# Splitting low parts on VectorE alone: GpSimd leaves tensor work in a two-layer attention, convolution and expert kernel

## The chip, the cores and the metric

The kernel runs on one core of a Trainium2 chip. The metric is the device time of one execution in microseconds, the median over runs. A change of under 0.2% (some 3.7 us) can hardly be told from no change.

## What is computed

Two layers over 256 tokens of width 1024, all in fp32. Each layer is a mixer (attention over one block of 256 keys and a gated convolution of width 3, their outputs gated, added and projected) and a mixture of single-vector experts (product keys, top 16 of 16384 experts for each of 8 heads). Every normalization has a scale and a shift that come from a vector `c`.

```python
for l in range(DEPTH):
    ada = (c @ w_ada[l] + b_ada[l])[:, None, :]
    sh1, sc1, g1, sh2, sc2, g2 = jnp.split(ada, 6, axis=-1)
    h = rmsnorm(x, norm1_g[l]) * (1.0 + sc1) + sh1
    q, k, v, b_gate, c_gate, hc, gate_a, gate_c = jnp.split(h @ w_in[l], SPLIT_POINTS, axis=-1)
    merged = (jax.nn.sigmoid(gate_a) * (moba_attention(q, k, v, slopes) @ w_attn_proj[l])
              + jax.nn.sigmoid(gate_c) * (gated_short_conv(b_gate, c_gate, hc, conv_w[l]) @ w_conv_proj[l]))
    x = x + g1 * (merged @ w_out[l])
    h = rmsnorm(x, norm2_g[l]) * (1.0 + sc2) + sh2
    x = x + g2 * peer(h, w_query[l], sub_keys[l], expert_u[l], expert_v[l])
return rmsnorm(x, final_g)
```

## The kernel before

**Order.** Everything is emitted by hand in one order (`manual_schedule`), and each engine takes its own instructions in that order, with semaphores between engines. All weights form one list, `stream`, of 1 MB groups of two units. `load_ahead` (L175) issues the groups on the SyncE queue, in order, as soon as a buffer is free: five buffers `raw0` for the first 13 groups, then a ring of three buffers `raw`, and in the expert stages parts of other tiles too.

**Mixers.** A mixer multiplies in two parts: each weight unit `raw` (128x1024) is split into a high part `wh`, written by ScalarE (L340), and a low part `wl = raw - wh` (L345); the activations are split into `hh` and `hl` likewise. TensorE then does three products, `wh*hh`, `wh*hl` and `wl*hh` (`step`, L392, and `across`, L818). `next_unit` (L311) prepares one unit, up to four units ahead of TensorE. `l_engine` (L304) says which engine takes the low part:

```python
pol["acc"] += pol["pool"]
if pol["acc"] >= 0.999:
    pol["acc"] -= 1.0
    return G
return V
```

So a share of 0.5 gives GpSimd (G) every second unit and VectorE (V) the rest. Between the weight groups `stream` holds groups of `w_ada`, which go to no matrix product: VectorE multiplies each unit with `c` and sums (L288), or adds it up with a factor (L285).

The first mixer begins with `first_norm` (L517), where the order is `START = "cuuccvcuccvcc"`: c is a pair of L288 units that ends in one column block of scale and shift, u and v are weight groups. After each c, `shift` (L531) lets ScalarE write `hh` and then `z`, and the low part `hl` is their difference (L536). In the second layer `norm` (L584) does this (L624). The stages of a mixer: query, key and value products, convolution, gates (L780), the projections (L797 to L801), the output product (`across`).

**Experts.** Tokens 0 to 127 go dense through all experts (`U` by L1099, `V` by L1157), with weights from one-hot factors: `onehots` (L1060) writes `q = (j == jT)` on VectorE (L1068) and multiplies it with `gT` (L1069), ScalarE writes `p`, TensorE multiplies (L1086), and VectorE applies the result (L1088). Four tokens are one batch, and a batch is used two batches after it is made. Tokens 128 to 255 fetch their expert rows one by one with indirect DMAs on the GpSimd queue (L991), and VectorE takes each row in (L1007, L1015).

At the end of a layer `finish_block` and `rstd` (L491) update `x` and work out its norms with a row of tiny VectorE instructions (L484 to L489); between them `next_unit` prepares the first units of the next layer.

Of the kernel before, what the change touches and what calls it, by code (L numbers as in the profile page):

```python
# [14 lines left out]
OP = mybir.AluOpType  # L15
# [4 lines left out]
KD = D // 128  # L20
# [4 lines left out]
TB = 4  # L25
# [10 lines left out]
WARM = (3, 6, 6)  # L36
LEAD = 4

POOL_START, POOL_MIX, POOL_PROJ = 0.5, (0.6, 0.4), 0.34


def f(ap):
    return ap.bitcast(F32)
# [3 lines left out]
def body(ctx: ExitStack, tc: tile.TileContext, d: dict, out: bass.AP):  # L47
    nc = tc.nc
    V, A, G, T = nc.vector, nc.scalar, nc.gpsimd, nc.tensor
# [20 lines left out]
    def w_ps(shape):  # L70
        return psum.tile(shape, F32, name="wp", bufs=2)

    def y_ps(shape):
        return psum.tile(shape, F32, name="yp", bufs=4)
# [227 lines left out]
    pol = {"pool": 0.0, "acc": 0.0}  # L302
# [78 lines left out]
    def unit(kind):  # L381
        n = AHEAD + (2 if more["pool"] is not None and kind != "out" else 0)
        while len(ready) < n + 1 and next_unit():
            pass
        return take(kind)

    def take(kind):
        k, h, lo = ready.popleft()
        assert k == kind, (k, kind)
        return h, lo  # L390
# [109 lines left out]
    def rms_row(between=lambda: None):  # L500

        dg = work.tile([128, NT, 128], F32, name="dg")
        y = rstd()
        for t in range(NT):
            if t:
                A.activation(dg[:, t], ident, AF.Copy, scale=y[:, t:t + 1])
            else:
                V.tensor_scalar(dg[:, t], ident, y[:, t:t + 1], None, op0=OP.mult)
        ps = y_ps([128, S])
        for t in range(NT):  # L510
            T.matmul(ps[:, t * 128:(t + 1) * 128], ones, dg[:, t], start=True, stop=True)
        between()
        rr = dg.rearrange("p t c -> p (t c)")
        V.tensor_copy(rr, ps)
        return rr

    def first_norm(xps):  # L517


        rr = rms_row(lambda: [next_unit() for _ in range(2)])  # L520
        for j in range(KD // 2):
            V.tensor_tensor(xh[:, 2 * j:2 * j + 2], xps[j], rr[:, None].to_broadcast([128, 2, S]), op=OP.mult)
        hh = split["h"].tile([128, KD, S], F32R, name="hh")
        hl = split["h"].tile([128, KD, S], F32R, name="hl")
        n = NFIRST[0]
        ws, reach, nv = [], [], 0
        pss = [(y_ps if i < 4 else mm_ps)([128, S]) for i in range(n)]
        vp = [w_ps([128, 512]) for _ in range(NT)]
        k = 0

        def shift(k):  # L531
            a, b = acol[:, 0, 0, k:k + 1], adac[:, 0, 0, k:k + 1]
            z = work.tile([128, S], F32, name="hf", bufs=4)
            A.activation(hh[:, k], xh[:, k], AF.Identity, bias=b, scale=a)
            A.activation(z, xh[:, k], AF.Identity, bias=b, scale=a)
            (V if k == KD - 1 else G).tensor_tensor(hl[:, k], z, f(hh[:, k]), op=OP.subtract)  # L536

        def products(nu, nk):
            new = [(i, x) for i in range(nu) for x in range(reach[i], nk)]
            for i, x in new:  # L540
                h, lo = (w[:, x * 128:(x + 1) * 128] for w in ws[i])
                T.matmul(pss[i], h, hh[:, x], start=(x == 0), stop=False)
                T.matmul(pss[i], lo, hh[:, x], start=False, stop=False)
            for i, x in new:
                h = ws[i][0][:, x * 128:(x + 1) * 128]
                T.matmul(pss[i], h, hl[:, x], start=False, stop=(x == KD - 1))
                reach[i] = x + 1

        todo = []
        while k < KD or len(ws) < n:  # L550
            for fn in todo:
                fn()
            todo = []
            next_unit()
            if ready and ready[0][0] == "qk":
                ws.append(take("qk"))
                reach.append(0)
            while k < KD and (0, 0, k) in done:
                shift(k)
                k += 1  # L560
            todo.append(lambda a=len(ws), b=k: products(a, b))
            while ready and ready[0][0] == "v" and k >= 2 * nv + 2:
                todo.append(lambda w=take("v"), u=nv: v_unit(vp, hh, hl, *w, u))
                nv += 1
        for fn in todo:
            fn()
        while nv < 4:
            v_unit(vp, hh, hl, *unit("v"), nv)
            nv += 1
        for _ in range(AHEAD + 1):  # L570
            next_unit()
        return hh, hl, pss, vp

    def v_unit(vp, hh, hl, h, lo, u):
        for kk in range(2):
            k = 2 * u + kk
            for t in range(NT):
                ts = slice(t * 128, (t + 1) * 128)
                c = slice(kk * 512, (kk + 1) * 512)
                T.matmul(vp[t], hh[:, k, ts], h[:, c], start=(k == 0), stop=False)  # L580
                T.matmul(vp[t], hh[:, k, ts], lo[:, c], start=False, stop=False)
                T.matmul(vp[t], hl[:, k, ts], h[:, c], start=False, stop=(k == KD - 1))

    def norm(l, w, kind, xps):  # L584

        rr = rms_row()
        keep_warm(WARM[2])
        hh = split["h"].tile([128, KD, S], F32R, name="hh")
        hl = split["h"].tile([128, KD, S], F32R, name="hl")
        ws, pss = [], []  # L590

        def products(k, low):
            if not ws:
                while len(ready) < 2:
                    next_unit()
                ws.extend(take(kind) for _ in range(2))
                pss.extend(y_ps([128, S]) for _ in range(2))
            c = slice(k * 128, (k + 1) * 128)
            for (h, lo), ps in zip(ws, pss):
                if low:  # L600
                    T.matmul(ps, h[:, c], hl[:, k], start=False, stop=(k == KD - 1))
                else:
                    T.matmul(ps, h[:, c], hh[:, k], start=(k == 0), stop=False)
                    T.matmul(ps, lo[:, c], hh[:, k], start=False, stop=False)

        def shift(k):
            z = work.tile([128, S], F32, name="hf", bufs=4)
            V.scalar_tensor_tensor(z, xps[k // 2][:, k % 2], acol[:, l, w, k:k + 1], rr, op0=OP.mult, op1=OP.mult)
            b = adac[:, l, 2 * w, k:k + 1]
            if k == 0:  # L610
                V.tensor_scalar(hh[:, k], z, b, None, op0=OP.add)
            else:
                A.activation(hh[:, k], z, AF.Identity, bias=b)
                if k % 2:
                    A.activation(z, z, AF.Identity, bias=b)
            return z, b

        zs = deque()
        for k in range(KD):
            while len(zs) < LEAD and k + len(zs) < KD:  # L620
                zs.append(shift(k + len(zs)))
            z, b = zs.popleft()
            if k % 2:
                G.tensor_tensor(hl[:, k], z, f(hh[:, k]), op=OP.subtract)  # L624
            else:
                V.scalar_tensor_tensor(hl[:, k], z, b, f(hh[:, k]), op0=OP.add, op1=OP.subtract)
            products(k, False)
            if k:
                products(k - 1, True)
        products(KD - 1, True)  # L630
        return hh, hl, pss
# [17 lines left out]
    def mixer(pool, l, hh, hl, pss, vp=None):  # L649
# [157 lines left out]
        for k in range(KD - 2):  # L807
# [3 lines left out]
                warm_sqrt()  # L811
            across(ys, mh[:, k], ml[:, k], h, lo, k == 0, False)
            tick()
        pol["pool"] = 1.0
        more["pool"] = None
        return finish(pool, ys, row, "out", [(mh[:, k], ml[:, k]) for k in (KD - 2, KD - 1)])

# [138 lines left out]
    def experts(es, xp, rp, low, halves, pairs, hot, l, hf, pss):  # L956
# [8 lines left out]
        gT = xp.tile([128, 128], F32, name="gT")  # L965
# [94 lines left out]
        def onehots(half, b):  # L1060


            x = b % 3
            p = hot[:, 2 * x:2 * x + 2].rearrange("p a b -> p (a b)").rearrange("p (t i) -> p t i", t=TB)
            q = hot[:, 6 + x].rearrange("p (t j) -> p t j", t=TB)
            ts = slice(b * TB, b * TB + TB)
            all_j = iotf[:, None, 64 * half:64 * half + 64].to_broadcast([128, TB, 64])
            V.tensor_tensor(q, all_j, jT[:, ts, None].to_broadcast([128, TB, 64]), op=OP.is_equal)  # L1068
            G.tensor_tensor(q, q, gT[:, ts, None].to_broadcast([128, TB, 64]), op=OP.mult)  # L1069
            for i in range(TB):  # L1070
                A.activation(p[:, i], iotf, AF.Abs, bias=iT[:, b * TB + i:b * TB + i + 1])  # L1071
            A.activation(p, p, AF.Relu, bias=1.0, scale=-1.0)
            return p, q
# [60 lines left out]
        for e in range(0, NE, 2):  # L1134
# [33 lines left out]
            if e == LAST:  # L1168
                assert not flying
                finish_block(1, 0)  # L1170
        pol["pool"] = 1.0
        finish_block(0, 0)
        if not xg:
            while len(ready) < 2 and next_unit():
# [110 lines left out]
```

## Time and profile before

| | |
|---|---|
| median of 3 runs | 1861.13 us (1859.49 to 1862.21) |
| the profiled execution's own time | 1862.17 us |
| its span, from the first instruction to the last | 1860.4 us |
| busy in the span | TensorE 1608.0, VectorE 1398.7, ScalarE 575.4, GpSimd 945.4 us |
| moved by DMA | 669.24 MB, mean 360 GB/s |

The two layers are at 0 to 945 and 945 to 1860 us. In each, a mixer of 210 to 250 us is followed by the query product (65 us), the U stage, of which the last 110 us have the one-hot weighting, and the V stage (300 us). PE is TensorE, DVE is VectorE, ACT is ScalarE, POOL is GpSimd, SP is SyncE, whose queue issues the weight loads. Busy time of an engine counts every instruction from its start to its end.

### The profile page before, as it was taken

The numbers are of one execution on the slowest core, as the hardware profiler recorded it, in microseconds if no ns is written. First come the engines' busy times: TensorE is split into PE (matmuls) and PEld (weight loads), VectorE is DVE, ScalarE is ACT, GpSimd is POOL, SyncE is SP. The second block draws the span as 40 slices with busy tenths as digits, with TensorE's granted clock in tenths as the row PEclk, the third lists the DMA queues.
The fourth block names the chain that finished last, engine by engine and source line by source line (L and its number), as shares of the span: only waits on it lengthen the run. The fifth ranks groups of instructions, "written<-read, shape, count | busy, mean of one in ns | idle before, by whom it ended". The sixth has DMA issues, their size and how long they took to land.

```text
span 1860.4 us, 26229 instructions
## 1 busy us (share of the span) xinstructions
PE 1608.0 (86%) x9527; PEld 1260.9 (68%) x9527; DVE 1398.7 (75%) x2681; ACT 575.4 (31%) x1257; POOL 945.4 (51%) x731
## 2 busy tenths in 40 slices
PE   6799989986789989887789999998786998898776
PEld 4788878986789644532357997898785994444222
DVE  7797859999988767654565877699997887666455
ACT  3464332111166433300046443221113653431001
POOL 3435204444589777755341231244446987776551
PEclk7899999988989999999999999999898999999998
DMA  8668788999999999999945677899999999999996
GB/s 318 249 227 298 295 341 298 408 409 409 408 391 395 411 415 415 415 415 415 397 178 199 252 291 263 328 377 408 409 408 394 392 404 416 414 415 412 416 416 271
DMA packets 163203, 669.24 MB, mean 360 GB/s; under 512 B 16001, under 2 KB 16001, under 8 KB 146690
## 3 DMA queue, kind: packets, MB, share of 16 engines
q1 hardware_dynamic: 87346, 396.39, 54.3%
q0 software_dynamic: 73856, 268.48, 36.4%
q10 hardware_dynamic: 1872, 2.69, 0.4%
q8 instruction: 75, 1.23, 0.3%
q14 instruction: 54, 0.44, 0.1%
HBM read 666.46 MB, written 1.05 MB: 359 GB/s over the span
## 4 chain that ended last, share of the span: by engine, by line
DVE 31%; DMA 27%; PE 24%; issue 8%; POOL 6%; ACT 3%; SPq 0%; POOLq 0%; DVEq 0%; ACTq 0%
DMA rows<-in_expert_v_dram,idx 15%; PE mm L1099 8%; DVE rows L1007 7%; DMA raw<-in_expert_v_dram 6%; PE yp L1157 4%; POOL rows L991 4%; PE wp L1086 3%; DVE raw L288 3%; DVE y L1015 3%; DMA rows<-in_expert_rows_dram,idx 2%; DVE wl L345 2%; PE mm L394 2%; PE mm L395 1%; PE mm L396 1%; ACT wh L340 1%
## 5 line engine op out<-in xcount | busy, mean ns | idle before, releaser
L991 POOL DMA_INDIRECT rows<-in_expert_rows_dram,idx x256 | 305.6, 1194 | 335.4 <-DVE rows L1007 90.4
L991 POOL DMA_INDIRECT rows<-in_expert_v_dram,idx x256 | 329.9, 1289 | 234.2 <-DMA rows<-in_expert_v_dram,idx 97.5
L1015 DVE SCALAR_TENSOR_TENSOR y<-rows,cv,y 128x1024 f32<-128x1024 f32 x254 | 335.1, 1319 | 146.8 <-DMA rows<-in_expert_v_dram,idx 140.4
L1007 DVE SCALAR_TENSOR_TENSOR rows<-rows,h 128x1024 f32<-128x1024 f32 x256 | 328.7, 1302 | 0.4 <-DMA rows<-in_expert_rows_dram,idx 0.3
L1157 PE MATMUL yp<-raw,ah 128*128 128x512 f32 x512 | 238.9, 613 | 60.6 <-DMA raw<-in_expert_v_dram 59.4
L345 POOL TENSOR_TENSOR wl<-raw,wh 128x1024 fp32r<-128x1024 f32 x52 | 136.1, 2622 | 267.0 <-ACT wh L340 255.4
L1157 PE MATMUL yp<-raw,al 128*128 128x512 f32 x512 | 241.1, 614 | 33.8 <-DMA raw<-in_expert_v_dram 33.0
L1099 PE MATMUL mm<-hfull,raw 128*128 128x128 f32 x1984 | 239.9, 280 | 20.0 <-ACT al L1113 16.8
L1099 PEld LDWEIGHTS mm<-hfull,raw 128*128 128x128 f32 x1984 | 231.1, 195 | 20.9 <-ACT al L1113 17.2
L1071 ACT ACTIVATE hot<-iotf,iT 128x128 f32<-128x128 f32 x512 | 163.2, 390 | 263.3 <-PE wp L1086 217.5
L1157 PEld LDWEIGHTS yp<-raw,ah 128*128 128x128 f32 x512 | 94.7, 193 | 203.2 <-DMA raw<-in_expert_v_dram 103.9
L1099 PE MATMUL mm<-hfull,ah 128*128 128x128 f32 x1600 | 192.8, 282 | 13.5 <-ACT al L1113 13.5
L1099 PEld LDWEIGHTS mm<-hfull,ah 128*128 128x128 f32 x1600 | 189.3, 199 | 13.8 <-ACT al L1113 13.8
L1157 PEld LDWEIGHTS yp<-raw,al 128*128 128x128 f32 x512 | 93.8, 193 | 138.0 <-issue 96.0
L394 PE MATMUL mm<-hh,wh 128*128 128x256 f32 x512 | 149.8, 293 | 12.3 <-ACT qT L658 6.8
L340 ACT ACTIVATE wh<-raw 128x1024 fp32r<-128x1024 f32 x112 | 116.0, 1052 | 115.9 <-DMA raw<-in_w_gt_dram 47.9
L1086 PEld LDWEIGHTS wp<-hot 128*128 128x128 f32 x1024 | 129.1, 192 | 31.9 <-issue 28.5
L1069 POOL TENSOR_TENSOR hot<-hot,gT 128x256 f32<-128x256 f32 x128 | 148.6, 1161 | 2.3
L395 PE MATMUL mm<-hl,wh 128*128 128x256 f32 x512 | 146.3, 286 | 0.0
L396 PE MATMUL mm<-hh,wl 128*128 128x256 f32 x512 | 146.1, 285 | 0.0
L1086 PE MATMUL wp<-hot 128*128 128x64 f32 x1024 | 128.3, 268 | 2.8 <-POOL hot L1069 2.8
L345 DVE TENSOR_TENSOR wl<-raw,wh 128x1024 fp32r<-128x1024 f32 x60 | 92.4, 1548 | 45.4 <-ACT wh L340 45.3
(230 smaller groups left out, 2346.4 us busy)
## 6 DMA issues: line engine op xcount, KB each, us to landing
raw<-in_expert_v_dram SPq DMA_DIRECT2D x128, 1024.0 KB
raw<-in_expert_u_dram SPq DMA_DIRECT2D x62, 1024.0 KB
ah<-in_expert_u_dram SPq DMA_DIRECT2D x50, 1024.0 KB
raw<-in_w_adat_dram SPq DMA_DIRECT2D x64, 512.0 KB
raw<-in_w_gt_dram SPq DMA_DIRECT2D x16, 1024.0 KB
raw<-in_w_adag_dram SPq DMA_DIRECT2D x16, 1024.0 KB
raw<-in_w_cv_dram SPq DMA_DIRECT2D x12, 1024.0 KB
raw<-in_w_qk_dram SPq DMA_DIRECT2D x8, 1024.0 KB
```

The lines of the kernel that those rows point to most:

```text
L345: l_engine().tensor_tensor(lo, raw, f(h), op=OP.subtract)
L394: T.matmul(ps, h[:, c], mh[:, k], start=first, stop=False)
L395: T.matmul(ps, h[:, c], ml[:, k], start=False, stop=False)
L396: T.matmul(ps, lo[:, c], mh[:, k], start=False, stop=last)
L991: G.indirect_dma_start(out=t, out_offset=None, in_=rows[kind], in_offset=bass.IndirectOffsetOnAxis(ap=idx[:, s:s + 1], axis=0))
L1007: V.scalar_tensor_tensor(t, t, 1.0, h1, op0=OP.mult, op1=OP.mult, accum_out=av[:, s:s + 1])
L1015: V.scalar_tensor_tensor(y1, t, cv[:, s:s + 1], y1, op0=OP.mult, op1=OP.add)
L1069: G.tensor_tensor(q, q, gT[:, ts, None].to_broadcast([128, TB, 64]), op=OP.mult)
L1071: A.activation(p[:, i], iotf, AF.Abs, bias=iT[:, b * TB + i:b * TB + i + 1])
L1086: T.matmul(ps[:, t], p[:, t], q[:, t], start=True, stop=True)
L1099: T.matmul(ps[:, u + x], raw[:, x, k * 128:(k + 1) * 128], hf[:, k, :128], start=(k == 0), stop=(k == KD - 1))
L1157: T.matmul(ys[q], halves[i // 64][:, i % 64], raw[:, x, q * 512:(q + 1) * 512], start=(i == 0), stop=(i == NE - 1))
```

## The change

The low parts that GpSimd made go to VectorE: the weights' (the three shares are 0, and so are the two places where the share was 1 at the end of a mixer and of the experts), those of `h` in both layers, and the multiplication of the one-hot factor with `gT`. GpSimd keeps the memsets, iotas and masks, its DMAs and the three products of the last normalization (L459). The order of emission is the same; what was queued on GpSimd stands at the same place of VectorE's queue.

```diff
-POOL_START, POOL_MIX, POOL_PROJ = 0.5, (0.6, 0.4), 0.34
+POOL_START, POOL_MIX, POOL_PROJ = 0.0, (0.0, 0.0), 0.0
...
-            (V if k == KD - 1 else G).tensor_tensor(hl[:, k], z, f(hh[:, k]), op=OP.subtract)
+            V.tensor_tensor(hl[:, k], z, f(hh[:, k]), op=OP.subtract)
...
             if k % 2:
-                G.tensor_tensor(hl[:, k], z, f(hh[:, k]), op=OP.subtract)
+                V.tensor_tensor(hl[:, k], z, f(hh[:, k]), op=OP.subtract)
...
-        pol["pool"] = 1.0
+        pol["pool"] = 0.0
         more["pool"] = None
...
             V.tensor_tensor(q, all_j, jT[:, ts, None].to_broadcast([128, TB, 64]), op=OP.is_equal)
-            G.tensor_tensor(q, q, gT[:, ts, None].to_broadcast([128, TB, 64]), op=OP.mult)
+            V.tensor_tensor(q, q, gT[:, ts, None].to_broadcast([128, TB, 64]), op=OP.mult)
...
-        pol["pool"] = 1.0
+        pol["pool"] = 0.0
         finish_block(0, 0)
```

## Rows read from the trace of the kernel before

**Rows 1.** Busy time by stage; after busy times the granted clock, DMA share, GB/s.

```profile
10.00:62.00 52.00, 34.97 (x180) 29.68 (x179) 43.31 (x63) 20.29 (x29) 21.78 (x12) 0.77 0.76 298
138.00:185.00 47.00, 42.13 (x343) 41.19 (x342) 33.54 (x23) 20.72 (x33) 24.49 (x9) 1.00 0.83 304
185.00:250.00 65.00, 57.28 (x325) 47.42 (x326) 52.43 (x73) 22.15 (x33) 13.44 (x5) 0.95 0.75 274
...
520.00:631.00 111.00, 110.95 (x952) 107.83 (x952) 94.30 (x149) 69.50 (x182) 97.91 (x79) 0.99 1.01 396
631.00:930.00 299.00, 250.44 (x737) 120.62 (x735) 180.22 (x277) 59.01 (x152) 180.87 (x143) 0.99 1.01 412
930.00:988.00 58.00, 45.73 (x216) 31.64 (x217) 36.96 (x48) 26.85 (x51) 21.60 (x18) 0.92 0.55 197
...
1121.00:1157.00 36.00, 32.77 (x145) 24.14 (x143) 26.69 (x34) 13.14 (x22) 5.46 (x2) 0.95 0.64 235
```

**Rows 2.** Waits of TensorE, 62 to 250 us: total, times, longest.

```profile
PE mm L394 <- ACT gt L780: 5.1, 4, 1.9
PE yp L824 <- DVE wl L345: 2.6, 2, 1.8
PE yp L824 <- POOL wl L345: 1.9, 1, 1.9
```

**Rows 3.** Lines L345, L288, L1068, L1069, L991: minimum, median, maximum in ns.

```profile
L345 DVE TENSOR_TENSOR wl<-raw,wh x60: 1207/1224/5683, 16.0 to 1144.2; 128x1024 fp32r<-128x1024 f32 x60
L345 POOL TENSOR_TENSOR wl<-raw,wh x52: 2342/2443/3450, 16.4 to 1133.9; 128x1024 fp32r<-128x1024 f32 x52
L288 DVE SCALAR_TENSOR_TENSOR raw<-raw,cbc x64: 1210/1219/3425, 10.4 to 1060.7; 128x1024 f32<-128x1024 f32 x64
L1068 DVE TENSOR_TENSOR hot<-iotf,jT x128: 409/418/837, 520.5 to 1694.2; 128x256 f32<-128x256 f32 x128
L1069 POOL TENSOR_TENSOR hot<-hot,gT x128: 619/1520/1702, 521.8 to 1696.4; 128x256 f32<-128x256 f32 x128
L991 POOL DMA_INDIRECT rows<-in_expert_v_dram,idx x256: 932/1414/1959, 440.5 to 1818.7; - x128
```

**Rows 4.** Groups of VectorE instructions: busy us, mean ns, idle before.

```profile
L288 DVE SCALAR_TENSOR_TENSOR raw<-raw,cbc 128x1024 f32<-128x1024 f32 x64 | 105.1, 1679 | 2.9 <-issue 1.6 <-DMA raw<-in_w_adat_dram 1.3
L345 DVE TENSOR_TENSOR wl<-raw,wh 128x1024 fp32r<-128x1024 f32 x60 | 92.4, 1548 | 45.4 <-ACT wh L340 45.3
```

**Rows 5.** Timeline of the start, three engines: start us, us, instruction.

```profile
30.61 1.22 DVE L345 TENSOR_TENSOR wl<-raw,wh 128x1024 fp32r<-128x1024 f32 x1 [2.11 <-ACT wh L340]
31.76 3.42 DVE L288 SCALAR_TENSOR_TENSOR raw<-raw,cbc 128x1024 f32<-128x1024 f32 x1
...
31.61 2.49 POOL L345 TENSOR_TENSOR wl<-raw,wh 128x1024 fp32r<-128x1024 f32 x1 [1.15 <-ACT wh L340]
...
25.97 0.59 ACT L535 ACTIVATE hf<-xh,adac,acol 128x256 f32<-128x256 f32 x1
```

**Rows 6.** Timeline of the layers' boundary, GpSimd, ScalarE and VectorE.

```profile
944.81 6.95 POOL L345 TENSOR_TENSOR wl<-raw,wh 128x1024 fp32r<-128x1024 f32 x3 [33.57 <-ACT wh L340]
...
943.69 1.99 ACT L340 ACTIVATE wh<-raw 128x1024 fp32r<-128x1024 f32 x2
...
949.50 2.26 DVE L489 SCALAR_TENSOR_TENSOR ss<-ss 128x2 f32<-128x2 f32 x1
951.80 0.28 DVE L508 TENSOR_SCALAR dg<-ident,ss 128x128 f32<-128x128 f32 x1
```

**Rows 7.** Timeline of VectorE and the SyncE queue in the second mixer.

```profile
966.28 10.15 DVE L345 TENSOR_TENSOR wl<-raw,wh 128x1024 fp32r<-128x1024 f32 x3 [1.09 <-ACT wh L340]
...
973.17 0.38 SPq L198 DMA_DIRECT2D raw<-in_w_qk_dram  x1
```

**Rows 8.** Waits of TensorE, 930 to 1157 us.

```profile
PE yp L678 <- ACT kT L656: 3.5, 1, 3.5
PE yp L824 <- DVE wl L345: 2.7, 1, 2.7
```

## The prediction

> **What bounds the kernel now.** I read first the busy time by stage [rows 1]. In the one-hot part of the U stage TensorE is busy 110.95 of 111 us, and in the V stage the 16 DMA engines have a share of 1.01 over 299 us: there an easier VectorE or GpSimd ends nothing sooner. The mixers are another thing. At the start (10 to 62 us) VectorE is the busiest engine, 43.3 of 52 us, with TensorE at 35.0. In the rest of the mixers TensorE has most of the time, but not all: 42.1 of 47 us in the gates, 57.3 of 65 in the projections and the output product of layer 0, 45.7 of 58 where layer 1 begins, 32.8 of 36 where its mixer ends. The DMA share is 0.55 to 0.83 there, so the weights are late because their buffers come free late, not because the DMA engines are full. So the question is what VectorE and GpSimd do to those gaps.
>
> The second view is the timeline of the start [rows 5]. GpSimd begins a low part at 31.61 and takes 2.49 us, until 34.10. VectorE begins an L288 at 31.76, and this takes 3.42 us where the median is 1.22 [rows 3]: it stood still until GpSimd had ended, and then took its own time. So VectorE does not work beside GpSimd here, it stands still for 2.2 us. The means show how common that is: 1679 ns against a median of 1219 for 64 L288, 1548 against 1224 for the 60 low parts that VectorE has already [rows 3, 4]. On these two lines alone 64 x 0.46 + 60 x 0.32 = 49 us are standstill.
>
> **The change, part by part.** *Load.* VectorE gets 52 low parts of weights, one start to the next 1.15 us (30.61 to 31.76, [rows 5]): 60 us. It gets 11 low parts of `h`, 128x256 with two inputs, as L1068 is, whose median is 0.42: 5 us. It loses at least the 49 us of standstill. So its busy time in the mixers stays about equal, by rows between -5 (if lines outside the two stand still as well) and +16 us of about 360. What changes is how late a low part is: 1.15 us in place of 2.44, and no neighbour of 3.4 us behind it. GpSimd loses 52 x 2.44 = 127 us that were hidden or blocked VectorE.
>
> *Start, -2.4 us.* Each low part moved here takes 2.2 us of standstill away and adds 1.15: -1.05. The first two weight groups hold two such parts and one `hl` of 0.4 comes in: -1.7. Four more groups have one each (v, u, v and the group behind START): -4.2. Against it stand the three places where a c follows a c. `hl` is now in VectorE's queue ahead of the next L288, and it waits for `z`, two activations of 0.59 on ScalarE [rows 5]; that L288 now starts at once. Three times 1.2: +3.5. Where a weight group follows, `hl` is free: VectorE waits 2.11 us for `wh` there anyway. Sum -2.4. Bounds: -6 if those waits fall into others, +3.5 if no low part stood on the path.
>
> *Gates of layer 0, -3.8.* A ring buffer is free when the low part of its second unit is done, 1.3 us (2.44 less 1.15) sooner than on GpSimd, and the `w_ada` units beside it stand still no more. A period of weight group and `w_ada` group has to be under the 5.9 us that TensorE needs for two units (42.13 us for 343 matmuls, of which two units have 48, [rows 1]); it is a little over it now, as the four waits of 5.1 us show [rows 2], put down to a ScalarE that itself waits for the load. I take three of the four away. Bounds 0 and -5.1.
>
> *Projections and output product of layer 0, -5.* TensorE waits for low parts 2.6 + 1.9 = 4.5 us [rows 2], and the granted clock is 0.95 over 65 us, 3.3 us of time at the higher level [rows 1]. VectorE has most to do here (52.4 of 65). I take the waits and a sixth of the clock. Bounds -1 and -7.8.
>
> *Layers' boundary, -2.* GpSimd makes three low parts from 944.81 to 951.76, and the tiny norm instructions stand still meanwhile: L489 takes 2.26 us, and L508 starts at 951.80 [rows 6]. Afterwards two low parts come ahead of these in VectorE's own queue: the two `wh` end at 945.68, so the second low part ends at about 947.1; then L484 and the root on ScalarE (0.4), the third `wh` (1.0) and its low part (1.15), and the last four tiny ones (0.8): 950.4, or -1.4. Low parts of `h` that VectorE needn't wait for give another -0.6. Bounds -3 and +1, if the third `wh` is later.
>
> *First loads of layer 1, -5.5.* Three low parts on VectorE take 10.15 us from 966.28 on, where 3.5 would be their time, and the load of the next key weights leaves at 973.17, right behind the second [rows 7]. TensorE then waits 3.5 us for the copy of `kT`, which stands behind that load in ScalarE's queue [rows 8]. If the parts that GpSimd makes among them go ahead on VectorE, and the three follow at 1.15 from 966.3 on, the load leaves at about 969.7. The wait goes, and of the clock, 0.92 over 58 us (4.6 us), I take 2 back. Bounds -2 and -8.1.
>
> *End of mixer 1, -2.* TensorE waits 2.7 us for a low part [rows 8]; 36 us at 0.95 hold 1.8 more. Bounds 0 and -4.5.
>
> *One-hot weighting, 0.* VectorE gets 128 products like L1068, 0.42 each, 54 us in four stretches, some 13 us in the 111 us stretch; it has 16.7 us left there, and L1068 itself is held up to 0.84 now [rows 1, 3]. The cover is TensorE (no gap) and then the DMA engines; without that cover it would cost 13 us. A batch is used two batches later, so what is behind the product in VectorE's queue (L1088, L1007) is later by 0.4, once each. Bounds -3 and +2.
>
> *GpSimd's queue.* Gathers no longer stand behind L1069 and its wait for L1068, memsets and masks no longer behind low parts. With a DMA share of 1.01 an earlier gather only waits longer in its queue: 0. The SyncE queue has the same loads in the same order; its waits for GpSimd become waits for VectorE.
>
> The sum: -2.4 -3.8 -5 -2 -5.5 -2 = -20.7 us. The profiled execution took 1862.17 us, so 1841.5; it stands 1.04 above the median of the runs, which gives 1840.4. I predict 1841.
>
> **A rule of the Trainium skill that speaks against it.** The gathers' issues take 932 ns at least and up to 1959 [rows 3], as if something held them too. The Trainium skill (SBUF — State Buffer, section "Who interferes with whom") says that a VectorE instruction with two SBUF inputs excludes a GpSimd instruction that reads SBUF, for the whole length of whichever came first. The standstill of 2.2 us agrees with it. By that rule the new products would hold up the gathers, if their issue reads its indices from SBUF; this is the third rival.
>
> **Rivals.**
> *Hidden gains.* TensorE bounds more of the mixers than its gaps say, because supply only shifts a gap to a later place. Then the start, the boundary and half of the first loads are left: -2.4 -2 -2.8, some 1854. For it: TensorE's busy share near 0.9. Against: each of the waits counted ends on a low part or a late load.
> *VectorE's queue as the bound (slower).* GpSimd took the waits for `wh` on itself; now each of the 46 moved parts that lie behind the start (52 less 6) can halt VectorE for up to one `wh`, 1.0 us, with the `w_ada` units behind it, whose buffers the next loads need. It decides from 0.45 us for each (20.7 / 46) on. At 0.7 it is +32 -21: 1872. For it: 45 us of idle time before VectorE's own 60 low parts, all for `wh` [rows 4]. Against: those waits cost little now, and up to four units stand ready.
> *Gathers held (slower).* 128 products of 0.42 each before a gather are 54 us, against at least 128 x 0.62 = 79 us that leave GpSimd [rows 3]. To count, half of the V stage's (64 products, 13 us) must delay a transfer that the stage waits for, with nothing given back: 1861 + 13 - 7 = 1867 with the hidden gains. Against: the share of 1.01.
> *No change.* The standstill is gone, but the mixers end with the same late loads: 1861.
> *More.* All gaps and the slow clock go in both mixers: -33, 1828.
>
> **How the numbers follow.** Forecast 0.57 (1833 to 1848), hidden gains 0.19, more 0.07, no change 0.07, VectorE's queue 0.06, gathers 0.04. Faster by over 0.2% (3.7 us, about what can be told from no change): 0.57 + 0.19 + 0.07 = 0.83; within 0.07; slower 0.10. The range 1830 to 1857 takes in the forecast, the hidden gains and the nearer part of "more". The slower cases hold one tenth, so no other range stands beside it.
>
> **What would show it.** Right: L288 and L345 have means within 5% of 1.22 us; no L345, L536, L624 or L1069 on GpSimd; VectorE's busy time about equal or lower; the tiny norm instructions at the boundary under 0.2 us each, and L508 some 1.4 us sooner behind the last square; no 3.5 us wait for `kT`; TensorE's waits for gates and low parts under 5 us in layer 0; the U and V stages as long as before to 3 us. Wrong: VectorE's idle time for `wh` grows by over 20 us and TensorE's waits with it (the queue), the V stage grows (the gathers), or the mixers are shorter and an expert stage longer by as much.

## The result, and the profile after

The changed kernel takes 1833.64 us (median of 4 runs, 1832.33 to 1836.1), the kernel before 1860.39 (4 runs): 26.75 us less, ratio 0.9856, 95% interval 0.9843 to 0.9869. The profiled execution took 1834.56 us, with a span of 1832.8. I had forecast 1841, in a range of 1830 to 1857. One execution of the writing kernel below ran at a granted clock of 0.652 and took 2258.95 us; that kernel's ratio goes by its three others (1833.52 to 1836.52 us).

First the stages of the profile after; the columns are those of [rows 1] (window, length, busy time of TensorE, of its weight loads, of VectorE, ScalarE and GpSimd, then granted clock, DMA share, GB/s), and each window is about the same stretch of work as there.

```profile
10.00:62.00 52.00, 35.08 (x185) 30.09 (x186) 41.15 (x75) 20.56 (x29) 0.00 (x0) 0.81 0.76 300
132.00:177.00 45.00, 45.00 (x373) 44.54 (x372) 37.81 (x36) 22.26 (x35) 0.00 (x0) 1.00 0.93 345
177.00:235.00 58.00, 53.74 (x323) 44.31 (x323) 48.62 (x75) 20.60 (x31) 0.00 (x0) 1.00 0.77 285
505.00:616.00 111.00, 110.92 (x950) 108.66 (x949) 91.67 (x176) 68.28 (x178) 51.79 (x46) 0.98 1.00 391
616.00:915.00 299.00, 251.37 (x738) 121.11 (x739) 184.38 (x313) 60.65 (x157) 157.35 (x117) 0.98 1.02 414
915.00:966.00 51.00, 44.47 (x210) 31.31 (x209) 31.37 (x51) 23.62 (x42) 1.14 (x4) 0.93 0.59 215
1096.00:1131.00 35.00, 33.48 (x165) 25.42 (x163) 26.68 (x37) 13.15 (x22) 0.00 (x0) 1.00 0.67 243
```

In the gates of layer 0 (second row) TensorE has no gap left, and the granted clock of the projections behind them went from 0.95 to 1.00. The two expert stages (rows four and five) are as full as before, and the table of stages below has them as long, to 1.7 us. In the start (first row) TensorE is no busier than it was: 35.08 against 34.97 of 52 us.

VectorE's groups, in the columns of [rows 4]:

```profile
L345 DVE TENSOR_TENSOR wl<-raw,wh 128x1024 fp32r<-128x1024 f32 x112 | 135.0, 1222 | 41.4 <-ACT wh L340 40.4 <-PE mm L396 0.6
L288 DVE SCALAR_TENSOR_TENSOR raw<-raw,cbc 128x1024 f32<-128x1024 f32 x64 | 75.8, 1223 | 0.0
L1069 DVE TENSOR_TENSOR hot<-hot,gT 128x256 f32<-128x256 f32 x128 | 54.4, 425 | 4.4
L1068 DVE TENSOR_TENSOR hot<-iotf,jT 128x256 f32<-128x256 f32 x128 | 53.9, 421 | 0.0
```

The standstill is gone: 1222 and 1223 ns are what the undisturbed instructions took [rows 3]. VectorE makes 52 low parts and 128 products more and still has no more to do: the page gives it 1390.8 us of busy time, 1398.7 before. Its idle time for `wh` fell from 45.3 us [rows 4] to 40.4.

TensorE's waits, as in [rows 2] (first fence, 62 to 235 us) and [rows 8] (second, 916 to 1131):

```profile
PE mm L394 <- ACT qT L658: 3.3, 1, 3.3
PE yp L824 <- DVE wl L345: 1.7, 4, 0.8
```

```profile
PE yp L511 <- DVE dg L508: 6.1, 2, 5.7
PE yp L824 <- DVE wl L345: 0.8, 1, 0.8
PE yp L678 <- ACT kT L656: 0.7, 1, 0.7
```

The waits for gates don't appear any more, those for low parts went from 4.5 to 1.7 us and from 2.7 to 0.8, and that for `kT` from 3.5 to 0.7. The longest of layer 1, for `dg` at the layers' boundary, went from 7.2 to 5.7. One wait that I had not counted, and that [rows 2] leaves out, shrank too, that for the copy of `qT`: 3.3 us after, and in TensorE's waits before (62 to 250 us)

```profile
PE mm L394 <- ACT qT L658: 6.8, 1, 6.8
```

In both kernels that copy stands in ScalarE's queue behind a `wh` (L340) that ScalarE sits idle before, 5.25 us in the one and 3.75 in the other. ScalarE's timeline before, then after (start us, us, instruction, idle before):

```profile
77.04 1.06 ACT L340 ACTIVATE wh<-raw 128x1024 fp32r<-128x1024 f32 x1 [5.25 <-DMA raw<-in_w_cv_dram]
78.00 0.37 ACT L658 ACTIVATE qT<-mm 128x256 f32<-128x256 f32 x1
```

```profile
72.91 1.06 ACT L340 ACTIVATE wh<-raw 128x1024 fp32r<-128x1024 f32 x1 [3.75 <-DVE raw L288]
73.87 0.37 ACT L658 ACTIVATE qT<-mm 128x256 f32<-128x256 f32 x1
```

The length of this wait depends on when TensorE comes to it as well: in the kernel below that moves the weights alone it is 6.0 us, behind a start that is 5.3 us shorter. What can be compared is when the copy comes: 78.00 us before and 73.87 after, 4.1 sooner.

Where the time came from, stage by stage: how much shorter (-) or longer (+) each is than in the profiled execution of before. A stage's end is the last V product of the start, the first and last sigmoid L780, the first L641, the last L1157, or the norm L608. "Again" is a second profile of the changed kernel, "late" an experiment below.

| stage | forecast | after | again | late |
|---|---|---|---|---|
| start, to the last V product (65.8 us before) | -2.4 | -0.6 | -2.2 | -2.2 |
| attention of layer 0, to the first sigmoid (139.9) | 0 | -5.9 | -5.2 | +0.4 |
| gates of layer 0 (to 186.4) | -3.8 | -2.9 | -2.8 | +1.7 |
| projections, output product, norm (to 249.9) | -5 | -5.8 | -5.9 | -0.9 |
| U and V of layer 0 (to 941.0) | 0 | +1.7 | +1.5 | -0.3 |
| layers' boundary (to 953.9) | -2 | -1.4 | -1.5 | -0.9 |
| first loads, attention of layer 1 (to 1057.8) | -5.5 | -7.9 | -8.1 | -6.7 |
| gates, projections, output of layer 1 (to 1156.4) | -2 | -3.1 | -3.1 | +2.8 |
| U and V of layer 1 (to 1850.4) | 0 | -1.7 | -1.6 | -2.7 |
| sum | -20.7 | -27.6 | -28.9 | -8.8 |

Executions of the same stage with the same code differ by 2 to 3 us (the kernel with the one-hot edit alone, below, has +3.3 up to the first L641, though its mixers are those of before). So no single entry of that size proves anything.

Now the two places that I had worked out by the instruction. VectorE in the start, for [rows 5]:

```profile
24.71 0.42 DVE L536 TENSOR_TENSOR hl<-hf,hh 128x256 fp32r<-128x256 f32 x1 [1.16 <-ACT hf L535]
...
28.98 0.42 DVE L536 TENSOR_TENSOR hl<-hf,hh 128x256 fp32r<-128x256 f32 x1 [1.16 <-ACT hf L535]
29.93 2.36 DVE L345 TENSOR_TENSOR wl<-raw,wh 128x1024 fp32r<-128x1024 f32 x2 [0.52 <-ACT wh L340]
32.20 1.22 DVE L288 SCALAR_TENSOR_TENSOR raw<-raw,cbc 128x1024 f32<-128x1024 f32 x1
```

The L288 of 3.42 us takes 1.22, and two low parts one behind the other take 2.36. The price stands in the brackets: each `hl` makes VectorE wait 1.16 us for its activation. At the layers' boundary, for [rows 6], ScalarE and VectorE:

```profile
930.23 1.99 ACT L340 ACTIVATE wh<-raw 128x1024 fp32r<-128x1024 f32 x2
...
931.31 2.36 DVE L345 TENSOR_TENSOR wl<-raw,wh 128x1024 fp32r<-128x1024 f32 x2 [1.80 <-ACT wh L340]
933.58 0.15 DVE L484 SCALAR_TENSOR_TENSOR ss<-ss 128x2 f32<-128x2 f32 x1
934.95 1.23 DVE L345 TENSOR_TENSOR wl<-raw,wh 128x1024 fp32r<-128x1024 f32 x1 [1.22 <-ACT wh L340]
...
936.68 0.16 DVE L489 SCALAR_TENSOR_TENSOR ss<-ss 128x2 f32<-128x2 f32 x1
936.88 0.29 DVE L508 TENSOR_SCALAR dg<-ident,ss 128x128 f32<-128x128 f32 x1
```

L489 takes 0.16 us in place of 2.26. From the `wh` pair, which begins when the last square has been read out, to L508 it is 936.88 - 930.23 = 6.65 us; before, 951.80 - 943.69 = 8.11 [rows 6]: 1.46 less, where I had worked out 1.4. What holds L508 now is the low part of the third `wh`, in front of it in VectorE's own queue.

In the first loads of layer 1, the low parts that took 10.15 us for three [rows 7] take

```profile
949.36 5.82 DVE L345 TENSOR_TENSOR wl<-raw,wh 128x1024 fp32r<-128x1024 f32 x5 [3.29 <-ACT wh L340]
...
955.20 0.38 SPq L198 DMA_DIRECT2D raw<-in_w_qk_dram  x1
```

5.82 us for five, and the load of the key weights leaves at 955.20 against 973.17: 18.0 us sooner, of which 14.9 had been gained up to the norm of layer 1, so 3.1 us here.

### The profile page after: what moved, and what is told of

It reads as the page before. It is cut to its first block, busy times and chain, and to the rows that moved or that the text cites. A ratio compares the mean times of both kernels' runs of the same rounds, so it can differ in the third digit from the quotient of the medians.

```text
span 1832.8 us, 26002 instructions
## 1 busy us (share of the span) xinstructions
PE 1600.5 (87%) x9527; PEld 1257.6 (69%) x9527; DVE 1390.8 (76%) x2872; ACT 577.5 (32%) x1257; POOL 634.9 (35%) x540
## 3 DMA queue, kind: packets, MB, share of 16 engines
q10 hardware_dynamic: 1872, 2.69, 0.4%
HBM read 666.46 MB, written 1.05 MB: 364 GB/s over the span
## 4 chain that ended last, share of the span: by engine, by line
DMA 33%; DVE 31%; PE 26%; issue 5%; ACT 3%; POOL 1%; SPq 0%; POOLq 0%; DVEq 0%; ACTq 0%
DMA rows<-in_expert_v_dram,idx 20%; DVE rows L1007 8%; PE mm L1099 8%; DMA rows<-in_expert_rows_dram,idx 5%; DMA raw<-in_expert_v_dram 5%; PE yp L1157 4%; PE wp L1086 3%; DVE y L1015 3%; PE mm L394 3%; DVE wl L345 2%; PE mm L395 2%; PE mm L396 2%; DVE raw L288 2%; ACT wh L340 1%; DVE ti L838 1%
## 5 line engine op out<-in xcount | busy, mean ns | idle before, releaser
L991 POOL DMA_INDIRECT rows<-in_expert_rows_dram,idx x256 | 292.2, 1142 | 783.3 <-PE mm L940 239.8
L1015 DVE SCALAR_TENSOR_TENSOR y<-rows,cv,y 128x1024 f32<-128x1024 f32 x254 | 325.7, 1282 | 161.2 <-DMA rows<-in_expert_v_dram,idx 156.4
L991 POOL DMA_INDIRECT rows<-in_expert_v_dram,idx x256 | 327.0, 1277 | 294.4 <-DMA rows<-in_expert_v_dram,idx 105.0
L1007 DVE SCALAR_TENSOR_TENSOR rows<-rows,h 128x1024 f32<-128x1024 f32 x256 | 307.5, 1217 | 19.4 <-DMA rows<-in_expert_rows_dram,idx 19.0
L1157 PE MATMUL yp<-raw,ah 128*128 128x512 f32 x512 | 240.8, 617 | 65.8 <-DMA raw<-in_expert_v_dram 64.6
L1157 PE MATMUL yp<-raw,al 128*128 128x512 f32 x512 | 239.3, 611 | 31.2 <-DMA raw<-in_expert_v_dram 30.3
L1157 PEld LDWEIGHTS yp<-raw,ah 128*128 128x128 f32 x512 | 95.3, 194 | 209.8 <-DMA raw<-in_expert_v_dram 108.2
L1157 PEld LDWEIGHTS yp<-raw,al 128*128 128x128 f32 x512 | 93.2, 192 | 134.2 <-issue 94.9
L345 DVE TENSOR_TENSOR wl<-raw,wh 128x1024 fp32r<-128x1024 f32 x112 | 135.0, 1222 | 41.4 <-ACT wh L340 40.4
L340 ACT ACTIVATE wh<-raw 128x1024 fp32r<-128x1024 f32 x112 | 115.8, 1052 | 70.7 <-DMA raw<-in_w_gt_dram 26.6
L394 PEld LDWEIGHTS mm<-hh,wh 128*128 128x128 f32 x512 | 99.2, 194 | 9.9 <-issue 4.0
L395 PEld LDWEIGHTS mm<-hl,wh 128*128 128x128 f32 x512 | 99.2, 194 | 0.0
```

The lines of the kernel that those rows point to most:

```text
L340: A.activation(h, raw, AF.Copy)
L345: l_engine().tensor_tensor(lo, raw, f(h), op=OP.subtract)
L394: T.matmul(ps, h[:, c], mh[:, k], start=first, stop=False)
L395: T.matmul(ps, h[:, c], ml[:, k], start=False, stop=False)
L991: G.indirect_dma_start(out=t, out_offset=None, in_=rows[kind], in_offset=bass.IndirectOffsetOnAxis(ap=idx[:, s:s + 1], axis=0))
L1007: V.scalar_tensor_tensor(t, t, 1.0, h1, op0=OP.mult, op1=OP.mult, accum_out=av[:, s:s + 1])
```

## The experiments

All times are against runs of the kernel before on the same chip (medians of 1858.67 to 1862.5 us).

**One part of the change alone.** First the kernel before with the shares alone set to zero (the `h` parts and L1069 stay on GpSimd):

```diff
-POOL_START, POOL_MIX, POOL_PROJ = 0.5, (0.6, 0.4), 0.34
+POOL_START, POOL_MIX, POOL_PROJ = 0.0, (0.0, 0.0), 0.0
...
-        pol["pool"] = 1.0
+        pol["pool"] = 0.0
...
-        pol["pool"] = 1.0
+        pol["pool"] = 0.0
```

> Of the change only the 52 low parts of weights go to VectorE; those of h and the one-hot product stay on GpSimd. Theory (the mixers gain from the weights' low parts, the one-hot product is covered): about 1834 to 1831, the c-c waits of 1.2 us for hl at the start are not paid, so 1 to 4 us under the whole change. Rival (the expert stages or hl carry a good part): 1840 or more.

Measured: 1831.33 us, ratio 0.9861 (0.9844 to 0.9879). The low parts of the weights are the whole gain. Second, the kernel before with the weighting alone moved:

```diff
-            G.tensor_tensor(q, q, gT[:, ts, None].to_broadcast([128, TB, 64]), op=OP.mult)
+            V.tensor_tensor(q, q, gT[:, ts, None].to_broadcast([128, TB, 64]), op=OP.mult)
```

> Of the change only the one-hot product goes to VectorE. Theory (covered by TensorE and then by the DMA engines): 1860 within 3 us, the U and V stages as long as before. Rival (GpSimd's queue or the gathers carry a part of the gain, or VectorE's 54 us cost something): away from 1860 by over 4 us, to either side.

Measured: 1859.56 us, ratio 1.0006 (0.9994 to 1.0018): nothing, as forecast. With L1069 on GpSimd (the first of the two kernels), L1068 takes 553 ns in the mean and L1007 1307; with L1069 on VectorE, 420 and 1216. So VectorE stood still in the expert stages too, and its end there is worth nothing, since TensorE and the DMA engines cover it.

**Does VectorE stand still, and for what?** The changed kernel, but wherever GpSimd used to make a low part it now works beside VectorE on a scratch tile. In one kernel it reads two SBUF tensors, as a low part does; in the other it reads one column and then only writes:

```diff
+    scr = cst.tile([128, D], BF, name="scr")
...
-        l_engine().tensor_tensor(lo, raw, f(h), op=OP.subtract)
+        V.tensor_tensor(lo, raw, f(h), op=OP.subtract)
+        if l_engine() is G:            # shares as in the kernel before
+            G.tensor_tensor(scr, cbc, f(h), op=OP.subtract)      # reading
+            # writing, in place of it:
+            G.tensor_copy(scr[:, 0:1], f(h)[:, 0:1])
+            for _ in range(2):
+                G.memset(scr, 0.0)
...
-            tmp = pool.tile([128, 512], F32, name="tmp", bufs=2)
+            tmp = pool.tile([128, 512], F32, name="tmp", bufs=1)
```

> The changed kernel, with a two-input GpSimd instruction of 128x1024 beside every low part that GpSimd had before; nothing waits for its result (the scratch buffer of the residual update is one in place of two). Standstill theory (VectorE stands still while GpSimd reads with it): the gain is gone, 1855 or more, L288 again with a mean over 1.5 us. Latency rival (the gain is that a low part is ready after 1.2 in place of 2.4 us): 1834 to 1840, since all low parts are VectorE's still.

> As the one with the two-input instruction beside, but GpSimd only reads one column of wh and then writes 128x1024 zeros twice. Theory (only a GpSimd instruction that reads excludes VectorE's two-input instructions): 1834 to 1837, L288 at 1.22 us. Rival (any GpSimd tensor work beside VectorE costs as much): near the run with the two-input instruction.

Measured: reading 1909.74 us, ratio 1.0277 (1.0258 to 1.0295); writing 1835.95, ratio 0.988 (0.9858 to 0.9902). The groups of the reading kernel, then of the writing one (L346 is the low part there):

```profile
L346 DVE TENSOR_TENSOR wl<-raw,wh 128x1024 fp32r<-128x1024 f32 x112 | 198.7, 1801 | 20.8 <-ACT wh L341 20.7
L288 DVE SCALAR_TENSOR_TENSOR raw<-raw,cbc 128x1024 f32<-128x1024 f32 x64 | 94.5, 1513 | 0.0
...
L348 POOL TENSOR_TENSOR scr<-cbc,wh 128x1024 bf16<-128x1024 f32 x52 | 150.6, 2896 | 348.2 <-ACT wh L341 342.9 <-ACT gt L783 5.0
```

```profile
L346 DVE TENSOR_TENSOR wl<-raw,wh 128x1024 fp32r<-128x1024 f32 x112 | 135.0, 1221 | 45.4 <-ACT wh L341 44.2 <-PE mm L401 0.6
L288 DVE SCALAR_TENSOR_TENSOR raw<-raw,cbc 128x1024 f32<-128x1024 f32 x64 | 75.5, 1218 | 0.0
...
L350 POOL MEMSET scr<- 128x1024 bf16 x104 | 99.0, 952 | 6.1
L348 POOL CAST scr<-wh 128x1 bf16<-128x1 f32 x52 | 36.9, 709 | 288.2 <-ACT wh L341 287.9
```

(The last line of the edit makes room for the scratch tile; the writing kernel has it too.) GpSimd is busy in both, for 150.6 and 135.9 us. Only where it reads do VectorE's two groups stand still, and 52 such reads make the kernel 76 us slower than the changed one, though nothing waits for what they make. That is more than the change gained. By their means the two groups stand still for 83 us here (112 x 0.58 + 64 x 0.29), 49 in the kernel before: a read begins with the same `wh` as VectorE's low part of that unit, and 42 of the 52 overlap a low part on VectorE in the trace, against 24 in the kernel before. VectorE also has 52 low parts more than there. GpSimd is held as well: its reads take 2896 ns in the mean and 2361 at least. The rule that I cited ahead (the Trainium skill, SBUF — State Buffer, "Who interferes with whom") also says that a GpSimd instruction that only writes does not contend with such a VectorE instruction; 1221 and 1218 ns beside 104 memsets agree.

**Is it the standstill, or that the low part is ready sooner?** The writing kernel with its scratch work put behind the low part, and a last step of it that makes the part's first column once more, so that TensorE and the next load wait for GpSimd:

```diff
-            G.tensor_copy(scr[:, 0:1], f(h)[:, 0:1])
-            for _ in range(2):
-                G.memset(scr, 0.0)
+            G.tensor_copy(scr[:, 0:1], f(lo)[:, 0:1])
+            G.memset(scr, 0.0)
+            G.tensor_tensor(lo[:, 0:1], raw[:, 0:1], f(h)[:, 0:1], op=OP.subtract)
```

> In the changed kernel every low part that GpSimd used to make is still made by VectorE in 1.22 us, but it counts as done later: GpSimd reads one column of it, fills a scratch tile (memset 128x1024, 0.95 us in the run with GpSimd writing) and then makes the part's first column once more; TensorE and the next load wait for that. By 0.23 to 0.71 us for each of the two one-column operations the part is 1.4 to 2.4 us later than in the changed kernel, where the kernel before had it 1.3 us later. So the lateness of the kernel before is there without its long reads. If the gain is the end of VectorE's standstill: at most 6 us above the run with GpSimd writing (1835.95), and L288 and the low part below 1.3 us in the mean. If the gain is the sooner low part: 1850 to 1865. In between, 1842 to 1850: both have a share, read off in proportion to the 26 us between the two kernels.

Measured: 1852.91 us, ratio 0.9959 (0.9945 to 0.9973). Its groups (L346 is the low part), and TensorE's waits from 62 to 250 us:

```profile
L346 DVE TENSOR_TENSOR wl<-raw,wh 128x1024 fp32r<-128x1024 f32 x112 | 135.0, 1222 | 48.7 <-ACT wh L341 44.9 <-PE mm L401 2.0 <-PE wp L401 1.6
L288 DVE SCALAR_TENSOR_TENSOR raw<-raw,cbc 128x1024 f32<-128x1024 f32 x64 | 75.6, 1219 | 0.9 <-DMA raw<-in_w_adat_dram 0.8
...
L349 POOL MEMSET scr<- 128x1024 bf16 x52 | 49.5, 952 | 3.1
L348 POOL CAST scr<-wl 128x1 bf16<-128x1 f32 x52 | 35.4, 681 | 340.8 <-DVE wl L346 319.2 <-DVE st L696 18.0 <-DVE zt L752 3.2
L350 POOL TENSOR_TENSOR wl<-raw,wh 128x1 fp32r<-128x1 f32 x52 | 20.1, 386 | 0.0
```

```profile
PE mm L399 <- ACT qT L663: 6.9, 1, 6.9
PE yp L829 <- POOL wl L350: 4.8, 2, 2.9
PE mm L399 <- ACT gt L785: 4.0, 4, 1.8
PE yp L829 <- DVE wl L346: 1.7, 1, 1.7
```

VectorE does not stand still here (1222 and 1219 ns), and yet the waits of the kernel before are back: four for gates, one of 6.9 us for `qT`, those for low parts. The start is as long as in "again" (-2.2), but the copy of `qT` comes at 75.86 us where it came at 73.88 there. So in layer 0 a late low part alone, by the ring buffers it keeps, can hold TensorE as long as before: of the 15.2 us that the mixer of layer 0 gained, 1.0 is left (column "late" of the table). In the first loads of layer 1 lateness costs little: -6.7 of -7.9 stay, which leaves the end of the standstill. The parts are 0.95 + 0.68 + 0.39 = 2.0 us later than VectorE makes them, though, where GpSimd's own were 1.2 us later (2.44 against 1.22, [rows 3]), so this kernel pays more for lateness than the kernel before did. Hence bounds: without the standstill and with parts later than ever it is still 0.41% faster than before, 7.6 us (5.0 to 10.2), the least that the end of the standstill is worth, if a later part never helps; what comes of sooner parts is then at most 26.8 - 7.6, some 19 us. Scaled by 1.2 / 2.0 that would be some 11.5, but no run shows that the cost grows in proportion. My expectation put a time above 1850 down to the sooner part alone; that is too much by these bounds.

**What the change costs.** More kernels on the changed one. In the first two, the low parts of `h` in the start go back to GpSimd, or are issued one unit later on VectorE, behind the next L288:

```diff
-            V.tensor_tensor(hl[:, k], z, f(hh[:, k]), op=OP.subtract)
+            (V if k == KD - 1 else G).tensor_tensor(hl[:, k], z, f(hh[:, k]), op=OP.subtract)
```

```diff
+            pend.append(lambda: V.tensor_tensor(hl[:, k], z, f(hh[:, k]), op=OP.subtract))
...
-            for fn in todo:
+            next_unit()
+            for fn in pend + todo:
                 fn()
+            pend.clear()
             todo = []
-            next_unit()
```

> The changed kernel with the first seven low parts of h of the start back on GpSimd. Theory (three places where a c follows a c cost 1.2 us each, since VectorE waits for z): 3 us under the changed kernel, 1831, and the start's last L536 some 3 us sooner. Rival (GpSimd's 0.74 us stand still behind L288 and hold VectorE up in turn): same as the changed kernel or slower.

> The changed kernel with each low part of h of the start emitted one unit later on VectorE, so that a product with w_ada runs while ScalarE writes z. Theory (the c-c waits are VectorE's order, not its load): 3.5 us under the changed kernel, and no wait of 1.16 us before L536. Rival (the start is held by the loads or by TensorE): no change.

Measured: on GpSimd 1830.16 us, ratio 0.9846 (0.9827 to 0.9866), with the start's last V product 5.3 us sooner than in the profile after and 3.7 sooner than in "again"; issued later 1832.04, ratio 0.9844 (0.9826 to 0.9863), with 3.4 and 1.8 us sooner. The waits of 1.16 us do lie on the path of the start. But TensorE waits for `qT` behind it: 5.4 us with the `h` parts on GpSimd where the kernel after had 3.3. By the end of layer 0's output product the first kernel has 3.6 us left of its 5.3, the second nothing of its 3.4. I had expected 3 and 3.5 us under the changed kernel; the intervals of all these ratios overlap, so neither gain is shown in the whole time.

In the third and fourth, the third weight unit of the boundary goes behind the whole norm, or the boundary's units go back to GpSimd:

```diff
-            if i == 1:
-                while 1 < len(ready) < 3 and next_unit():
-                    pass
...
-        rr = rms_row()
+        def third():
+            while 1 < len(ready) < 3 and next_unit():
+                pass
+
+        rr = rms_row(third)
```

```diff
-        pol["pool"] = 0.0
+        pol["pool"] = 1.0
         finish_block(0, 0)
```

> The changed kernel with the third unit of the layers' boundary prepared behind the matmuls of the norm row in place of between the root and the reciprocal. Theory (at the boundary VectorE's own queue now holds the norm: 1.2 us of waiting for wh and 1.15 of low part stand ahead of the reciprocal): 2 us under the changed kernel. Rival (TensorE has work enough, or the third unit is late for the value product): no change.

> The changed kernel with the low parts of the layers' boundary back on GpSimd (share 1 behind the experts, until the mixer sets it). Theory (GpSimd holds up the tiny norm instructions more than VectorE's own low parts do): 1.4 us over the changed kernel, and L487 to L489 again at 1 to 2.3 us each. Rival (VectorE's waits for wh cost as much as the standstill): no change.

Measured: 1831.27 us, ratio 0.9851 (0.9828 to 0.9875), and 1831.93, ratio 0.9854 (0.9832 to 0.9877). In the profiles the boundary is 1.2 us shorter in the one and 2.1 us longer in the other than after. In the latter the tiny norm instructions stand still once more, beside three low parts on GpSimd that take 6.95 us:

```profile
929.96 2.27 DVE L488 TENSOR_TENSOR ss<-ss 128x2 f32<-128x2 f32 x1
932.26 2.26 DVE L489 SCALAR_TENSOR_TENSOR ss<-ss 128x2 f32<-128x2 f32 x1
```

Neither can be seen in the whole time, where I had expected -2 and +1.4 us. Last, the changed kernel again, the two edits on VectorE together, and the one that takes `h` to GpSimd together with the later third unit, all on one chip:

> The changed kernel itself, for comparison with the two beside it: 1831 to 1835.

> The changed kernel with both orders mended on VectorE: the low parts of h of the start one unit later, and the third unit of the layers' boundary behind the norm row. Theory (two waits of VectorE's order, 3.5 and 2 us, and both are on the way to the end): 5 us under the changed kernel, 1828. Rival (the start's gain is lost again before the gates, as the profile of the first alone has it): 2 us under it.

> The changed kernel with the start's first seven low parts of h on GpSimd and the third unit of the layers' boundary behind the norm row. Theory: 5 us under the changed kernel, 1828, as the start's 3 us and the boundary's 2 us add. Rival (differences between executions of the same code in the first mixer are as large): within 2 us of the changed kernel.

Measured: 1834.44 us, ratio 0.986 (0.9841 to 0.9879); 1832.26, ratio 0.9839 (0.982 to 0.9858); 1831.68, ratio 0.9841 (0.9821 to 0.9861). The two are 2 to 3 us below the changed kernel where I had expected 5, and the intervals overlap: no version is shown to beat it, and local gains of 3.5 and 1.2 us did not add up at the end.

## Why the prediction was right, and where it was off

The mechanism held: the gain is the low parts of the weights, the one-hot weighting costs nothing, VectorE's standstill is gone, and the gaps that I named closed or shrank. What was off is the size, -26.8 against -20.7 us: my sum had nothing for the attention of layer 0, which gave -5.9 and -5.2. By its terms:

- *Start, -2.4*: -0.6 and -2.2 in two profiles, not to be told from the forecast. Its two halves stand apart in the runs that leave `h` on GpSimd: they have -5.9, -5.9 and -6.1, which is my sum without the 3.5 for the waits of `hl`. Where a weight group follows, `hl` is free as I had it: 1.16 + 0.52 us of waiting stand there in place of 2.11 [rows 5].
- *Gates of layer 0, -3.8*: here and in the attention ahead of them is most of the miss. All four waits went (5.1 us), not three, but the stage gave 2.9, as the first of the four (1.5 us) lies mostly ahead of the first sigmoid and so counts to the attention. There the wait for `qT` fell by 3.5 us, or by 1.9 in the second profile (4.9 us), whose start was 1.6 shorter: in both, start and wait together gave 4.1. I had not priced that wait at all, though it was the longest of layer 0's mixer. Attention and gates together gave -8.8 and -8.0. The run with late parts brings the waits for gates back (4.0 us) and the copy of `qT` 2.0 us later than "again", so the reason given for the gates, buffers that are free sooner, holds and covers `qT` as well. Another 1.4 to 2.3 us of the attention is no wait that the trace names.
- *Projections and output product, -5*: -5.8. The waits for low parts fell from 4.5 to 1.7 us, and the clock gave more than the sixth that I took: it is at 1.00 over the whole stretch, where it was 0.95.
- *Boundary, -2*: -1.4, the norm's part to the tenth; the 0.6 for `hl` does not show.
- *First loads of layer 1, -5.5*: -7.9. The load left 3.1 us sooner (worked out: 3.5), the `kT` wait went to 0.7; the rest is not one wait that the trace names. In the stage TensorE's idle time fell from 5.1 to 1.2 us and its busy time from 98.8 to 94.9, with a granted clock of 0.96 before and 0.98 after.
- *End of mixer 1, -2*: -3.1; *one-hot, 0*: 0.
- *VectorE's load, between -5 and +16 us in the mixers*: over the table's stages outside the experts its busy time fell from 357 to 345 us, beyond my bound. Lines that I had not counted stood still before as well: L764, which reads one tensor, has a median of 353 ns and took 2.24 us beside a low part of GpSimd at 92.15.

The rivals: *hidden gains* (1854) falls, since no stage gave back more than the 1.7 us of U and V in layer 0, which layer 1 returned; only a still shorter start (the `h` parts issued later) was lost again. *VectorE's queue* (1872) falls, with its idle time for `wh` at 40.4 us where it had to grow by over 20. *Gathers held* (1867) falls: L991 on the V stage's rows has 935, 1412 and 1932 ns (minimum, median, maximum) with 128 products more beside it, as before [rows 3]. *More* (1828) is 5.6 us from the measured time and the forecast 7.4, whose own band (1833 to 1848) holds it by 0.6; but *more* had all gaps and the slow clock go in both mixers, and 3.3 us of `qT`, 1.7 of low parts and a clock of 0.95 in the attention are left.

What stays open: the split between standstill and sooner parts inside the bounds above (7.6 us at least for the one, 19 at most for the other), and whether the waits of `hl` and the third unit are worth the 2 to 3 us that the last kernels hint at.

## What to carry to other kernels

An engine that takes work off another is no help if both stop each other: compare the mean with the median of the instructions beside it, and ask which of its instructions read SBUF while the other reads two tensors. Then price a helper's lateness by the buffer it holds, not by its own waits: a part that was 2.0 us later, with no standstill at all, cost TensorE waits for low parts, and for gates and `qT`, which the trace put down to ScalarE. List every wait of the bounding engine in the stage, the longest first, and say of each whether the change moves its cause.

## What the runs showed of the hardware

The exclusion goes both ways and does not look at size. In the kernel with late parts, GpSimd copies a single column beside an L288, and again while VectorE is idle:

```profile
32.14 1.22 DVE L288 SCALAR_TENSOR_TENSOR raw<-raw,cbc 128x1024 f32<-128x1024 f32 x1
32.35 1.05 POOL L348 CAST scr<-wl 128x1 bf16<-128x1 f32 x1 [9.21 <-DVE wl L346]
...
152.89 0.19 POOL L348 CAST scr<-wl 128x1 bf16<-128x1 f32 x1 [3.52 <-DVE wl L346]
```

Beside the L288 the copy ends only when that does, 1.05 us in place of 0.19. The other way round, VectorE's instructions on 128x2 elements took 2.26 us at the boundary in place of 0.16.

A memset on GpSimd kept its 952 ns and cost VectorE's two groups nothing, but it is not free for every VectorE instruction. In the writing kernel L769 (L764 of the kernel before), a tensor_scalar with one input in SBUF, has a median of 353 ns; three of the eight ran beside memsets, and each took 0.83 us:

```profile
1024.36 1.99 POOL L350 MEMSET scr<- 128x1024 bf16 x2
1024.62 0.83 DVE L769 TENSOR_SCALAR yc<-zt,cw 128x256 f32<-128x256 f32 x1
```

So the number of inputs alone does not tell what GpSimd can hold up.
